# A hybrid encoder block on one core: the norm of attention B from split squares, first loads on two queues, rotary products and splits pinned in program order

## The chip, the cores and the metric

The kernel runs on one core of a Trainium2 chip. The core has five engines with a stream of instructions each: TensorE (PE, matrix products), VectorE (DVE), ScalarE (ACT, functions from tables and casts), GpSimd (POOL) and SyncE (SP, here only the issuing of transfers). Each works through its stream in order and waits for the others by semaphores. The metric is the device time of one execution in microseconds.

## The reference

For a sequence of 512 rows of 1024 numbers: a combined projection, two attention mixers, a gate, an output product and a layer norm (LN1), then an MLP and a second norm. What the change touches is cut out here.

```
proj = x @ w_in -> q_a | k_a | v_a | q_b | k_b | v_b | gate logits
A: 8 heads of 64, chunked softmax attention with a relative bias
B: 4 heads; partial_rope on q_b and k_b (16 of 64 columns, with cos and sin);
   p = softmax(q1 k1^T) - lam * softmax(q2 k2^T), 128-row blocks, causal by chunks
   out = p @ v                                       # 128 columns a head
   out = out * rsqrt(mean(out^2) + 1e-5) * g * (1 - lam_init)
mix = (sigmoid(g_a) * (o_a @ w_a) + sigmoid(g_b) * (o_b @ w_b)) @ w_out
x = LN1(alpha * x + mix)
x = LN2(alpha * x + relu(x @ w_ff1)^2 @ w_ff2)
```

All is float32, and the products have to keep more than one pass of the fast float type (FR, fp32r) gives. So each operand is split in a high part h (a cast by ACT) and the rest l = src - h (a subtraction, mostly by DVE), and a product is three passes: h h, h l, l h.

## The kernel before

**Tiles and stages.** x comes transposed, in eight tiles of 128x512 (X, split into h and l). The weights are streamed in 512 KB chunks (`raw`), each split into `wh` and `wl`. `prefetch(n_dma, n_split)` issues the loads up to chunk n_dma and the splits up to n_split; `chunk()` hands out the next one. `s_group` multiplies four row tiles by 512 columns of weights, `t_pair` makes the transposed product. PE's work on weights comes from the generator `proj`; two more generators, `attn_a` and `attn_b`, give the steps of the attentions, and the main program interleaves them: 36 steps of A with one step of `proj` each, then the steps of B with 1.8 steps of `proj` each.

**Order.** A scheduler gives each engine its order from the dependences and its own estimates. It may move an instruction ahead of others, unless `tc.keep_in_program_order` holds that instruction at its place in the program.

**Attention B.** Each of the four heads has four units, t = 0 to 3, of 128 to 512 key columns. In a unit, `scores` (L270, L271) makes two score maps, DVE adds the mask and finds the maximum (L278), ACT takes the exponential with its row sum (L280), DVE the reciprocal of the sum (L282) and that times lambda (L574); POOL multiplies the second map (L575), and DVE subtracts (L576). PE transposes the result three units later (L289). After unit t = 1 the program has `rope` for q and k of the next head, four POOL products each (L480 to L485), and after t = 2 `prep_b`, in which PE transposes that head's q and k, four blocks each (L492). A unit's scores thus follow on the previous head's `prep_b`.

**The norm of B.** `pv` makes a head's output o (transposed, 128 dimensions by 512 rows); ACT writes its square (L516) and the gained output og (L518). Three steps later `mean_sq` sums the squares over the dimensions with sixteen narrow f32 matmuls in all (L524), and DVE finds 1/sqrt by three Newton steps on 128x8 tiles (L527 to L538). Six steps later `normalise` has POOL spread the result along diagonals (L547), PE multiplies these by ones, and DVE multiplies og by the product (L554).

**Attention A** has the same units with eight heads, where POOL's product is L372. **LN1** follows on the output product (L178 to L185 in groups named mm, o and st): DVE adds the residual (L735), takes statistics (L739), ACT and DVE normalise (L805, L806), and PE transposes (L817).

Of the kernel before, what the change touches and what calls it, by code (L numbers as in the profile page):

```python
# [9 lines left out]
F32 = mybir.dt.float32  # L10
# [30 lines left out]
def block_kernel(ctx, tc, w, x_t, x, pos, relb, bgate, lq1, lk1, lq2, lk2, subg,  # L41
# [36 lines left out]
    def o_bank():  # L78
        return bank("o")

    def split(src, h, l, eng=None):
# [6 lines left out]
    def load_x(k, cuts=((0, S),)):  # L88
        if k not in x_raw:
            x_raw[k] = e_tile()  # L90
        for lo, hi in cuts:
            nc.sync.dma_start(out=x_raw[k][:, lo:hi], in_=x_t[k * P:(k + 1) * P, lo:hi])

# [11 lines left out]
    dma_at, split_at = [0], [0]  # L105

    def prefetch(n_dma, n_split):
        while dma_at[0] < min(NCH, n_dma):
            i = dma_at[0]
            raws[i] = wp.tile([P, 1024], F32, tag="raw", bufs=3, name=name("raw"))  # L110
            if i == 0:
                for j in range(2):
                    sl = slice(512 * j, 512 * (j + 1))
                    if j == 0:
                        load_x(0, ((0, P),))
                    nc.sync.dma_start(out=raws[i][:, sl], in_=w[i][:, sl])
                    load_x(j, ((P, S),) if j == 0 else ((0, S),))
            else:
                nc.sync.dma_start(out=raws[i], in_=w[i])
            dma_at[0] += 1  # L120
        while split_at[0] < min(NCH, n_split):
            i = split_at[0]
            if i in dest:
                hs, ls = dest[i]
                for j in range(2):
                    split(raws[i][:, 512 * j:512 * (j + 1)], hs[j], ls[j],
                          G if i in on_pool else V)
                parts[i] = (hs, ls)
            else:
                h = wp.tile([P, 1024], FR, tag="wh", bufs=3, name=name("wh"))  # L130
                l = wp.tile([P, 1024], FR, tag="wl", bufs=3, name=name("wl"))
                if i == 0:
# [11 lines left out]
    def chunk(ahead=2):  # L144
        c = next_chunk[0]
        prefetch(c + ahead + 1, c + ahead)
        next_chunk[0] += 1
        return parts.pop(c)
# [6 lines left out]
    ones_r = const.tile([P, P], FR, name="ones_r")  # L155
    A.activation(ones_r, ones, AF.Copy, scale=128.0)
    epst = const.tile([P, 1], F32, name="epst")
# [28 lines left out]

    def s_group(act_h, act_l, evac, before=None, nk=4, tail=1, cut_last=False):

# [12 lines left out]
        for c in range(nk):  # L201
            if before:
                before(c)
            wh, wl = chunk()
# [35 lines left out]
    def warm_up(n):  # L240
        ps = st_bank()
        src = e_tile()
        V.memset(src, 0.0)
        for _ in range(n):
            T.matmul(ps, src[:, 0:P].bitcast(FR), src.bitcast(FR), start=True, stop=True)

# [250 lines left out]
    def attn_b():  # L497
# [3 lines left out]
        for which in range(2):  # L501
            rope(qb[which][0])
        ops[0] = prep_b(0)
        yield

        def pv(h):
# [3 lines left out]
            for j in range(NT):  # L510
# [8 lines left out]
            return og, sq  # L519

        def mean_sq(og, sq):
            ms = mm_bank()
            for t in range(NT):
                T.matmul(ms[:, 2 * t:2 * t + 2], sq[:, t * P:(t + 1) * P], ones[:, 0:2],  # L524
                         start=True, stop=True)
            v, y, a = small(8), small(8), small(8)
            V.tensor_scalar(v, ms[:, 0:8], EPS, None, op0=ALU.add)  # L527
            V.tensor_scalar(y.bitcast(I32), v.bitcast(I32), -0.5, float(0x5f3759df),
                            op0=ALU.mult, op1=ALU.add)
            for _ in range(3):  # L530
                V.scalar_tensor_tensor(out=a, in0=y, scalar=-0.5, in1=y,
                                       op0=ALU.mult, op1=ALU.mult)
                V.tensor_tensor(out=a, in0=a, in1=v, op=ALU.mult)
                V.scalar_tensor_tensor(out=y, in0=a, scalar=1.5, in1=y,
                                       op0=ALU.add, op1=ALU.mult)
            rh, rl = small(8, FR), small(8, FR)
            V.tensor_copy(out=rh, in_=y)
            V.tensor_tensor(out=rl, in0=y, in1=rh.bitcast(F32), op=ALU.subtract)  # L538
            return og, sq, rh, rl

        def normalise(og, a, rh, rl):
            rb = mm_bank()
            for n, part in enumerate((rh, rl)):
                diag = vt()
                r = part.bitcast(F32)
                eye = ident[:, :]
                G.tensor_tensor(out=diag.rearrange("p (t q) -> p t q", q=P),  # L547
                                in0=bass.AP(tensor=eye.tensor, offset=eye.offset,
                                            ap=[eye.ap[0], [0, NT], [1, P]]),
                                in1=bass.AP(tensor=r.tensor, offset=r.offset,  # L550
                                            ap=[r.ap[0], [2, NT], [0, P]]), op=ALU.mult)
                T.matmul(rb, ones_r, diag, start=(n == 0), stop=(n == 1))

            V.tensor_tensor(out=a.rearrange("p (q n) -> p n q", n=NT),  # L554
                            in0=og.rearrange("p (n q) -> p n q", q=P),
                            in1=rb.rearrange("p (n q) -> p n q", q=P), op=ALU.mult)
            h_, l_ = vt(), vt()
            split(a, h_, l_)
            ob_h.append(h_)
            ob_l.append(l_)  # L560

        held = {}
        for i in range(len(units) + LAG + 7):
            if i < len(units):
# [19 lines left out]
            if i >= LAG and i - LAG < len(units):  # L584
# [3 lines left out]
                prob_transpose(ex, t, *bufs[h], mm_bank)  # L588
            for stage in (6, 3, 1):
                k = i - LAG - stage  # L590
                if 0 <= k < len(units) and k % NT == NT - 1:
                    h = units[k][0]
                    if stage == 1:
                        held[h] = pv(h)
                    elif stage == 3:
                        held[h] = mean_sq(*held[h])
                    else:
                        normalise(*held.pop(h))
# [48 lines left out]
    def proj():  # L647
        def before(c):
            if c:
                for k in (2 * c, 2 * c + 1):  # L650
                    load_x(k)
                    split_x(k)
# [9 lines left out]

    A.preload_act_table(AF.Exp)
    warm_up(6)
    prefetch(1, 0)
    rope_angles()
    main = proj()
# [4 lines left out]

    advance(7)
    rope_tables()
# [13 lines left out]
    for _ in range(16 + LAG + 7):  # L688
        next(steps_b, None)
# [145 lines left out]
    for n, _ in enumerate(s_group(mh, ml, evac_res(0))):  # L835
        prefetch(c0 + 5, min(c0 + 3, next_chunk[0] + 3))
# [149 lines left out]
```

## Time and profile before

| | |
|---|---|
| median of three runs | 741.46 us (741.35 to 741.72) |
| profiled execution | 741.43 us |
| its span, first to last instruction | 739.6 us |
| mean granted clock of PE | 0.997 |
| busy: PE, DVE, ACT, POOL | 98%, 57%, 38%, 13% |
| read from memory, written | 71.45 MB, 2.10 MB |

A row of the profile names a line of the kernel, an engine, the operation, the tile written and those read. "Idle before" is the time for which the engine stood still just before those instructions, and the arrow names what ended it. Idle time of an engine for which nobody waits costs nothing.

### The profile page before, as it was taken

How to read it: one execution, taken by the hardware profiler on the slowest of the kernel's cores; microseconds unless marked ns; L12 is line 12 of the kernel's file. 1: busy time of each engine (PE TensorE's matmuls, PEld its weight loads, DVE VectorE, ACT ScalarE, POOL GpSimd, SP SyncE). 2: the span in 40 equal slices, each digit the busy share in tenths (PEclk: the TensorE clock that was granted, in tenths of full speed). 3: DMA queues.
4: the chain of work that ended last, by engine and by line, in shares of the span. 5: the costliest groups of instructions: out<-in, count | busy, mean ns of one | idle time of the engine just before them, and what ended most of it. 6: DMA issues, size and time to landing. Idle time of an engine off the chain costs nothing.

```text
span 739.6 us, 9267 instructions
## 1 busy us (share of the span) xinstructions
PE 725.7 (98%) x3446; PEld 606.0 (82%) x3446; DVE 423.4 (57%) x831; ACT 283.6 (38%) x497; POOL 94.4 (13%) x127
## 2 busy tenths in 40 slices
PE   8999999999999999999999999999999999999995
PEld 6888888878888888888788888888888888888885
DVE  6566655546666764746876886423135655612545
ACT  5565654536565643224363223221212322312200
POOL 0023333550122121143000000000000000000001
PEclk9999999999999999999999999999999999999998
DMA  8553222212332222182502232322223223232302
GB/s 294 197 173 112 85 88 60 83 58 86 121 108 86 86 63 104 62 313 96 190 1 84 87 114 86 115 86 98 102 86 113 86 86 113 86 113 86 115 29 85
DMA packets 26940, 78.34 MB, mean 106 GB/s; under 512 B 4368, under 2 KB 5136, under 8 KB 26896
## 3 DMA queue, kind: packets, MB, share of 16 engines
q1 hardware_dynamic: 26176, 76.71, 31.3%
q10 hardware_dynamic: 720, 1.05, 0.4%
q8 instruction: 27, 0.44, 0.2%
q14 instruction: 17, 0.14, 0.1%
HBM read 71.45 MB, written 2.10 MB: 99 GB/s over the span
## 4 chain that ended last, share of the span: by engine, by line
PE 87%; DVE 4%; POOL 3%; ACT 2%; DMA 2%; issue 1%; SPq 0%; DVEq 0%; ACTq 0%; POOLq 0%
PE mm L178 11%; PE mm L180 11%; PE mm L179 11%; PE mm L183 7%; PE mm L185 7%; PE mm L184 7%; PE st L185 3%; PE st L184 3%; PE st L183 3%; PE st L180 3%; PE st L179 3%; PE st L178 3%; POOL G L629 2%; DMA raw<-in_w_dram 2%; PE st L271 1%; PE o L185 1%
## 5 line engine op out<-in xcount | busy, mean ns | idle before, releaser
L83 DVE TENSOR_TENSOR wl<-raw,wh 128x1024 fp32r<-128x1024 f32 (+1 forms) x115 | 140.2, 1219 | 128.5 <-ACT wh L82 128.4
L82 ACT CAST wh<-raw 128x1024 fp32r<-128x1024 f32 (+1 forms) x115 | 120.0, 1044 | 207.6 <-PE st L185 67.1
L183 PE MATMUL mm<-wh,X 128*128 128x512 f32 (+1 forms) x192 | 77.0, 401 | 1.9 <-ACT X L82 1.6
L178 PE MATMUL mm<-X,wh 128*128 128x512 f32 x192 | 76.9, 401 | 0.0
L179 PE MATMUL mm<-X,wh 128*128 128x512 f32 x192 | 74.9, 390 | 0.0
L180 PE MATMUL mm<-X,wl 128*128 128x512 f32 x192 | 74.9, 390 | 0.0
L184 PE MATMUL mm<-wl,X 128*128 128x512 f32 (+1 forms) x192 | 74.5, 388 | 0.0
L185 PE MATMUL mm<-wh,X 128*128 128x512 f32 (+1 forms) x192 | 74.2, 388 | 0.0
L783 POOL TENSOR_SCALAR s<-s 128x1 f32<-128x1 f32 x1 | 0.4, 409 | 388.8 <-DVE s L767 388.8
L178 PE MATMUL mm<-x1t_h,wh 128*128 128x512 f32 x128 | 49.8, 389 | 0.0
L179 PE MATMUL mm<-x1t_l,wh 128*128 128x512 f32 x128 | 49.8, 389 | 0.0
L180 PE MATMUL mm<-x1t_h,wl 128*128 128x512 f32 x128 | 49.8, 389 | 0.0
L280 ACT ACTIVATE e<-e,s 128x128 f32<-128x128 f32 (+3 forms) x64 | 36.1, 564 | 30.4 <-DVE s L278 30.0
L372 POOL TENSOR_SCALAR e<-e,s 128x128 f32<-128x128 f32 (+3 forms) x32 | 34.7, 1085 | 76.3 <-DVE s L282 76.3
L183 PEld LDWEIGHTS mm<-wh,X 128*128 128x128 f32 x192 | 36.2, 189 | 9.8 <-ACT X L82 2.7
L185 PEld LDWEIGHTS mm<-wh,X 128*128 128x128 f32 x192 | 36.0, 188 | 7.8 <-DVE X L83 0.3
L180 PEld LDWEIGHTS mm<-X,wl 128*128 128x128 f32 x192 | 36.0, 188 | 7.7
L178 PEld LDWEIGHTS mm<-X,wh 128*128 128x128 f32 x192 | 36.1, 188 | 6.9
L184 PEld LDWEIGHTS mm<-wl,X 128*128 128x128 f32 x192 | 36.2, 188 | 6.7 <-DVE wl L83 0.2
L179 PEld LDWEIGHTS mm<-X,wh 128*128 128x128 f32 x192 | 36.2, 188 | 6.5
L82 ACT CAST V<-lt 128x512 fp32r<-128x512 f32 x24 | 14.9, 621 | 62.8 <-DVE lt L858 62.8
L180 PE MATMUL st<-x1t_h,wl 128*128 128x512 f32 (+1 forms) x104 | 38.8, 373 | 0.0
(257 smaller groups left out, 1537.0 us busy)
## 6 DMA issues: line engine op xcount, KB each, us to landing
raw<-in_w_dram SPq DMA_DIRECT2D x119, 512.0 KB, 3.3
q<-q SPq DMA_DIRECT2D x32, 128.0 KB, 2.3
G<-in_relb_dram SPq DMA_DIRECT2D x8, 256.0 KB, 4.2
x<-in_x_dram SPq DMA_DIRECT2D x4, 512.0 KB, 7.6
e<-in_x_t_dram SPq DMA_DIRECT2D x7, 256.0 KB, 6.4
out_dram<-x SPq DMA_DIRECT2D x3, 256.0 KB, 2.0
out_dram<-x ACTq DMA_DIRECT2D x3, 256.0 KB, 2.1
raw<-in_w_dram SPq DMA_DIRECT2D x2, 256.0 KB, 3.2
```

Of the source, the lines that this page charges most:

```text
L82: A.copy(out=h, in_=src)
L83: (eng or V).tensor_tensor(out=l, in0=src, in1=h.bitcast(F32), op=ALU.subtract)
L178: T.matmul(ps, lw_h, rh, start=first, stop=False)
L179: T.matmul(ps, lw_h, rl, start=False, stop=False)
L180: T.matmul(ps, lw_l, rh, start=False, stop=last)
L183: T.matmul(ps, ah, w_h, start=first, stop=False)
L184: T.matmul(ps, ah, w_l, start=False, stop=False)
L185: T.matmul(ps, al, w_h, start=False, stop=last)
L271: T.matmul(ps[:, :n], q2[:, sl], k1[:, :n], start=False, stop=True)
L280: A.activation(e[:, :n], e[:, :n], AF.Exp, bias=nm, scale=-1.0, accum_out=sums)
L372: G.tensor_scalar(ex[:, :n], ex[:, :n], r, None, op0=ALU.mult)
L629: G.tensor_tensor(out=m, in0=m, in1=g, op=ALU.add)
```

## The change

It has four parts.

1. *Norm of B.* `mean_sq` goes. In `pv` ACT squares o twice, once to f32 and once to FR, and DVE subtracts the two (`sq_h`, `sq_l`). `normalise` multiplies these by ones (of 1/128, in FR; one matmul each), which leaves the mean in every partition; ACT takes its square root with the epsilon as bias, and DVE the reciprocal over 128x512. The output product by it goes to a new tile. Exp and Sqrt lie in different table sets, so that ACT loads a table ahead of each change. The step comes three steps after `pv`'s in place of six after the unit, and there are three steps fewer at the end.
2. *First loads.* `first_loads` issues x tiles 0 and 1 from ACT's queue, ahead of its table load, and the halves of chunks 0 and 1 with x tiles 2 and 3 from SP's. Chunk 1 is split in halves too. The matmuls that warm PE up read a 128x128 tile repeatedly. `rope_angles` comes after two steps of `proj`.
3. *Rotary products.* The first of the four products of a `rope` call keeps its program order, and the two calls for head 0 become a step each, at i = 22 and 30.
4. *Splits in LN1.* The chunks needed next are split one by one behind the residual add and norm of each row tile, held in program order.

```
     def split(src, h, l, eng=None):
         A.copy(out=h, in_=src)
-        (eng or V).tensor_tensor(out=l, in0=src, in1=h.bitcast(F32), op=ALU.subtract)
+        i = (eng or V).tensor_tensor(out=l, in0=src, in1=h.bitcast(F32), op=ALU.subtract)
+        if pinned[0]:
+            tc.keep_in_program_order(i)
...
+    def first_loads():
+
+        load_x(0, ((0, P), (P, S)), A)
+        load_x(1, q=A)
+        for i in range(2):
+            raws[i] = wp.tile([P, 1024], F32, tag="raw", bufs=3, name=name("raw"))
+            for j in range(2):
+                sl = slice(512 * j, 512 * (j + 1))
+                nc.sync.dma_start(out=raws[i][:, sl], in_=w[i][:, sl])
+                if i == 1:
+                    load_x(2 + j)
+        dma_at[0] = 2
...
-                if i == 0:
+                if i < 2:
                     for j in range(2):
                         sl = slice(512 * j, 512 * (j + 1))
                         split(raws[i][:, sl], h[:, sl], l[:, sl])
-                        split_x(j)
+                        split_x(2 * i + j)
...
-        G.tensor_tensor(out=a, in0=v[:, :, :, 0:16], in1=cos_t, op=ALU.mult)
+        tc.keep_in_program_order(
+            G.tensor_tensor(out=a, in0=v[:, :, :, 0:16], in1=cos_t, op=ALU.mult))
...
         for which in range(2):
             rope(qb[which][0])
+            yield
         ops[0] = prep_b(0)
         yield
...
-            sq = e_tile()
+            sq, sq_h, sq_l = e_tile(), vt(), vt()
             A.activation(sq, o, AF.Square)
+            A.activation(sq_h, o, AF.Square)
             og = e_tile()
             A.activation(og, o, AF.Copy, scale=g8)
+            V.tensor_tensor(out=sq_l, in0=sq, in1=sq_h.bitcast(F32), op=ALU.subtract)
+            return og, sq, sq_h, sq_l
...
-        def mean_sq(og, sq):
-            ms = mm_bank()
-            for t in range(NT):
-                T.matmul(ms[:, 2 * t:2 * t + 2], sq[:, t * P:(t + 1) * P], ones[:, 0:2],
-                         start=True, stop=True)
...
+        def normalise(og, a, sq_h, sq_l):
             rb = mm_bank()
...
+            for n, part in enumerate((sq_h, sq_l)):
+                T.matmul(rb, ones_r, part, start=(n == 0), stop=(n == 1))
+            A.activation(a, rb, AF.Sqrt, bias=epst)
+            V.reciprocal(a, a)
+
+            b = e_tile()
+            V.tensor_tensor(out=b.rearrange("p (q n) -> p n q", n=NT),
                             in0=og.rearrange("p (n q) -> p n q", q=P),
-                            in1=rb.rearrange("p (n q) -> p n q", q=P), op=ALU.mult)
+                            in1=a.rearrange("p (n q) -> p n q", q=P), op=ALU.mult)
...
-            for stage in (6, 3, 1):
+            for stage in (3, 1):
...
-    A.preload_act_table(AF.Exp)
     warm_up(6)
-    prefetch(1, 0)
-    rope_angles()
+    first_loads()
+    tc.keep_in_program_order(A.preload_act_table(AF.Exp))
...
-        if i == 32:
+        if i in (22, 30, 32):
             next(steps_b)
...
+        pinned[0] = True
+        prefetch(c0 + 7, c0 + 4 + min(s + 1, 3))
+        pinned[0] = False
-    for _ in s_group(mh, ml, fin1, tail=4):
+    for _ in s_group(mh, ml, fin1, tail=4, ahead=0):
```

Line numbers shift with it: of the lines named above, L270/L271 become L278/L279, L278 L286, L280 L288, L282 L290, L372 L380, L480 to L485 L489 to L494, L492 L501, L554 L542, L574 L562, L575 L563, L576 L564, L735 L725, L739 L729, L805 L795, L817 L807.

Two places show the new order. Heads are counted from 0 here. The first is POOL's order in attention B, from unit t = 0 of head 1 on. In a row `e` is the second map of a unit (its column count stands last), `G` a head's q or k, and `s` small tiles. Before:

```order
L575 TENSOR_SCALAR e_2124<-e_2124,s_2131 128x128
L575 TENSOR_SCALAR e_2192<-e_2192,s_2199 128x256
L575 TENSOR_SCALAR e_2248<-e_2248,s_2255 128x384
L575 TENSOR_SCALAR e_2334<-e_2334,s_2341 128x512
L575 TENSOR_SCALAR e_2420<-e_2420,s_2427 128x128
```

And after the change:

```order
L563 TENSOR_SCALAR e_2127<-e_2127,s_2134 128x128
L563 TENSOR_SCALAR e_2195<-e_2195,s_2202 128x256
L489 TENSOR_TENSOR s_2206<-G_1186,cos_t 128x128
L490 TENSOR_TENSOR s_2207<-G_1186,sin_t 128x8x8
L492 TENSOR_TENSOR s_2207<-G_1186,sin_t 128x8x8
L494 TENSOR_TENSOR G_1186<-s_2206,s_2207 128x8x16
L489 TENSOR_TENSOR s_2212<-G_1499,cos_t 128x128
L490 TENSOR_TENSOR s_2213<-G_1499,sin_t 128x8x8
L492 TENSOR_TENSOR s_2213<-G_1499,sin_t 128x8x8
L494 TENSOR_TENSOR G_1499<-s_2212,s_2213 128x8x16
L563 TENSOR_SCALAR e_2251<-e_2251,s_2258 128x384
```

The eight rotary products of the next head, all of which stood ahead of attention B before, now stand behind the product of unit t = 1.

The second place is ACT's order at unit t = 1 of head 2, with the two exponentials of the unit, the casts of transposed maps (`ph`), the gates' function (`G`) and, after the change, the norm of head 0. Before:

```order
L607 ACTIVATE G_2461<-mm_2436,bg 128x512
L280 ACTIVATE e_2466,s_2468<-e_2466,s_2467 128x256
L296 CAST ph_2345<-mm_2499 128x3x128
L280 ACTIVATE e_2476,s_2478<-e_2476,s_2477 128x256
L607 ACTIVATE G_2565<-mm_2540,bg 128x512
```

And after:

```order
L593 ACTIVATE G_2468<-mm_2443,bg 128x512
L288 ACTIVATE e_2473,s_2475<-e_2473,s_2474 128x256
L304 CAST ph_2348<-mm_2506 128x3x128
L538 ACT_TABLE_LOAD
L538 ACTIVATE e_2367<-mm_2512,epst 128x512
L288 ACT_TABLE_LOAD
L288 ACTIVATE e_2483,s_2485<-e_2483,s_2484 128x256
L593 ACTIVATE G_2560<-mm_2535,bg 128x512
```

Two table loads and the square root of the norm now stand between the two exponentials. At the same place DVE's order, with the row-sum reciprocals (L290), the reciprocal of the norm (L539) and the product (L542) ahead of the unit's L562, is this after the change:

```order
L290 RECIPROCAL s_2478<-s_2475 128x1
L286 ISA e_2483,s_2484<-st_2480,maskb 128x256
L286 ISA s_2484 128x1
L305 TENSOR_TENSOR pl_2349<-mm_2506,ph_2348 128x3x128
L539 RECIPROCAL e_2367<-e_2367 128x512
L290 RECIPROCAL s_2488<-s_2485 128x1
L542 TENSOR_TENSOR e_2517<-e_2372,e_2367 128x4x128
L562 TENSOR_SCALAR s_2490<-s_2488,lam 128x1
```

Before, small instructions of `mean_sq` stood there:

```order
L282 RECIPROCAL s_2481<-s_2478 128x1
L528 TENSOR_SCALAR s_2511<-s_2510 128x8
L574 TENSOR_SCALAR s_2483<-s_2481,lam 128x1
L531 SCALAR_TENSOR_TENSOR s_2512<-s_2511 128x8
L533 TENSOR_TENSOR s_2512<-s_2512,s_2510 128x8
```

So L562, which POOL's product waits for, has the two wide instructions of the norm ahead of it.

## Rows read from the trace of the kernel before

**Rows 1.** The page: busy us (share of the span) xinstructions

```profile
PE 725.7 (98%) x3446; PEld 606.0 (82%) x3446; DVE 423.4 (57%) x831; ACT 283.6 (38%) x497; POOL 94.4 (13%) x127
```

**Rows 2.** PE's waits: engine, line, released by: us, times, longest

```profile
PE mm L183 <- ACT X L82: 1.6, 1, 1.6
...
PE st L289 <- POOL e L372: 1.3, 1, 1.3
PE mm L817 <- ACT lt L805: 1.0, 1, 1.0
...
PE o L352 <- DVE pl L297: 0.2, 1, 0.2
```

**Rows 3.** Groups of instructions: count | busy us, mean ns | idle before

```profile
L524 PE MATMUL mm<-ones,e 128*128 128x2 f32 x32 | 3.8, 241 | 0.0
```

**Rows 4.** Timeline, 0 to 13: start us, us, engine, line, tiles [idle before]

```profile
3.41 0.62 ACT L82 CAST wh<-raw 128x512 fp32r<-128x512 f32 x1 [1.08 <-DMA raw<-in_w_dram]
...
10.48 1.04 ACT L82 CAST wh<-raw 128x1024 fp32r<-128x1024 f32 x1 [0.60 <-DMA raw<-in_w_dram]
...
12.10 0.50 PE L183 MATMUL mm<-wh,X 128*128 128x512 f32 x1 [1.61 <-ACT X L82]
```

**Rows 5.** Timeline of POOL, 139 to 156

```profile
144.84 0.46 POOL L480 TENSOR_TENSOR s<-G,cos_t 128x128 f32<-128x128 f32 x1
...
146.47 0.46 POOL L480 TENSOR_TENSOR s<-G,cos_t 128x128 f32<-128x128 f32 x1
...
151.32 0.60 POOL L372 TENSOR_SCALAR e<-e,s 128x128 f32<-128x128 f32 x1
```

**Rows 6.** Timeline of DVE in LN1, 350 to 376

```profile
355.54 2.46 DVE L83 TENSOR_TENSOR wl<-raw,wh 128x1024 fp32r<-128x1024 f32 x2 [0.78 <-ACT wh L82]
...
362.69 1.21 DVE L83 TENSOR_TENSOR wl<-raw,wh 128x1024 fp32r<-128x1024 f32 x1
...
373.73 0.69 DVE L735 SCALAR_TENSOR_TENSOR x<-x,st 128x512 f32<-128x512 f32 x1 [1.48 <-PE st L185]
```

**Rows 7.** Timeline of PE: last scores of t = 1, and L492

```profile
175.96 0.28 PE L271 MATMUL st<-q,q 128*128 128x256 f32 x1
...
181.56 1.03 PE L492 MATMUL mm<-ident,G 128*128 128x128 f32 x8
...
200.84 0.28 PE L271 MATMUL st<-q,q 128*128 128x256 f32 x1
...
204.74 1.03 PE L492 MATMUL mm<-ident,G 128*128 128x128 f32 x8
...
226.41 0.28 PE L271 MATMUL st<-q,q 128*128 128x256 f32 x1
```

**Rows 8.** Timeline of POOL in attention B, 172 to 235

```profile
180.87 0.93 POOL L575 TENSOR_SCALAR e<-e,s 128x256 f32<-128x256 f32 x1 [2.18 <-PE mm L179]
...
204.70 0.93 POOL L575 TENSOR_SCALAR e<-e,s 128x256 f32<-128x256 f32 x1 [4.48 <-PE st L271]
...
230.07 0.92 POOL L575 TENSOR_SCALAR e<-e,s 128x256 f32<-128x256 f32 x1 [5.86 <-DVE s L531]
```

**Rows 9.** Timeline of ACT at a table load, 21 to 25

```profile
22.74 1.28 ACT L429 ACT_TABLE_LOAD   x1 [2.79 <-DVE ld L421]
24.03 0.32 ACT L429 ACTIVATE cos_t<-ld,halfpi 128x32 f32<-128x32 f32 x1
```

**Rows 10.** Timeline of ACT, second exponential of t = 1, head 2

```profile
228.83 0.51 ACT L280 ACTIVATE e<-e,s 128x256 f32<-128x256 f32 x1 [0.31 <-DVE s L278]
```

**Rows 11.** Groups of instructions on DVE with 128x512 elements

```profile
L858 DVE TENSOR_TENSOR lt<-lt 128x512 f32<-128x512 f32 x32 | 22.1, 692 | 1.1
...
L554 DVE TENSOR_TENSOR e<-e,mm 128x512 f32<-128x512 f32 x4 | 4.2, 1062 | 0.0
```

**Rows 12.** Timeline of PE, its last matmul

```profile
731.41 0.28 PE L185 MATMUL o<-wh,X 128*128 128x256 f32 x1
```

**Rows 13.** Stretches: us, busy of PE to POOL, PE clock, DMA share, GB/s

```profile
735.28:739.60 4.32, 0.00 (x0) 0.00 (x0) 0.98 (x2) 0.00 (x0) 0.64 (x1) 0.50 0.34 113
```

More of the change, by code (lines that the diff above doesn't have):

```diff
@@ L79, in o_bank, with load_x @@
         return bank("o")
+    pinned = [False]
     def split(src, h, l, eng=None):
         A.copy(out=h, in_=src)
-        (eng or V).tensor_tensor(out=l, in0=src, in1=h.bitcast(F32), op=ALU.subtract)
+        i = (eng or V).tensor_tensor(out=l, in0=src, in1=h.bitcast(F32), op=ALU.subtract)
+        if pinned[0]:
+            tc.keep_in_program_order(i)
     xh, xl, x_raw = [], [], {}
-    def load_x(k, cuts=((0, S),)):
-        if k not in x_raw:
-            x_raw[k] = e_tile()
+    def load_x(k, cuts=((0, S),), q=nc.sync):
+        x_raw[k] = e_tile()
         for lo, hi in cuts:
-            nc.sync.dma_start(out=x_raw[k][:, lo:hi], in_=x_t[k * P:(k + 1) * P, lo:hi])
+            q.dma_start(out=x_raw[k][:, lo:hi], in_=x_t[k * P:(k + 1) * P, lo:hi])
     def split_x(k):
@@ L110, in prefetch @@
             raws[i] = wp.tile([P, 1024], F32, tag="raw", bufs=3, name=name("raw"))
-            if i == 0:
[L112 to L119, printed above, removed]
+            nc.sync.dma_start(out=raws[i], in_=w[i])
             dma_at[0] += 1
@@ L145, in chunk @@
         c = next_chunk[0]
-        prefetch(c + ahead + 1, c + ahead)
+        prefetch(c + ahead + 1, c + max(ahead, 1))
         next_chunk[0] += 1
@@ L155, in block_kernel @@
     ones_r = const.tile([P, P], FR, name="ones_r")
-    A.activation(ones_r, ones, AF.Copy, scale=128.0)
     epst = const.tile([P, 1], F32, name="epst")
@@ L185, in smm, with s_group @@
         T.matmul(ps, al, w_h, start=False, stop=last)
-    def s_group(act_h, act_l, evac, before=None, nk=4, tail=1, cut_last=False):
+    def s_group(act_h, act_l, evac, before=None, nk=4, tail=1, cut_last=False, ahead=2):
         jobs = [(s, 0, S) for s in range(NT)]
@@ L203, in s_group @@
                 before(c)
-            wh, wl = chunk()
+            wh, wl = chunk(ahead)
             if c >= nk - tail:
@@ L241, in warm_up @@
         ps = st_bank()
-        src = e_tile()
-        V.memset(src, 0.0)
+        src = e_tile()[:, 0:P].bitcast(FR)
+        V.memset(src.bitcast(F32), 0.0)
+        wide = bass.AP(tensor=src.tensor, offset=src.offset, ap=[src.ap[0], [0, NT], [1, P]])
         for _ in range(n):
-            T.matmul(ps, src[:, 0:P].bitcast(FR), src.bitcast(FR), start=True, stop=True)
+            T.matmul(ps.rearrange("p (a b) -> p a b", b=P), src, wide, start=True, stop=True)
     def stack(ps, scale):
@@ L514, in pv @@
                          stop=(j == NT - 1))
-            sq = e_tile()
+            sq, sq_h, sq_l = e_tile(), vt(), vt()
             A.activation(sq, o, AF.Square)
+            A.activation(sq_h, o, AF.Square)
             og = e_tile()
             A.activation(og, o, AF.Copy, scale=g8)
-            return og, sq
-        def mean_sq(og, sq):
-            ms = mm_bank()
-            for t in range(NT):
-                T.matmul(ms[:, 2 * t:2 * t + 2], sq[:, t * P:(t + 1) * P], ones[:, 0:2],
-                         start=True, stop=True)
[L526 to L539, printed above, removed]
@@ L541, in normalise @@
-        def normalise(og, a, rh, rl):
-            rb = mm_bank()
[L543 to L554, printed above, removed]
+            V.tensor_tensor(out=sq_l, in0=sq, in1=sq_h.bitcast(F32), op=ALU.subtract)
@@ L557, in normalise @@
             h_, l_ = vt(), vt()
-            split(a, h_, l_)
+            split(b, h_, l_)
             ob_h.append(h_)
@@ L562, in attn_b @@
         held = {}
-        for i in range(len(units) + LAG + 7):
+        for i in range(len(units) + LAG + 4):
             if i < len(units):
@@ L648, in before @@
         def before(c):
-            if c:
+            for k in (2 * c + 2, 2 * c + 3):
+                if 0 < c and k < KD:
+                    load_x(k)
+            if c > 1:
                 for k in (2 * c, 2 * c + 1):
-                    load_x(k)
                     split_x(k)
@@ L661, in proj @@
         yield from branch(0, oa_h, oa_l)
-    A.preload_act_table(AF.Exp)
     warm_up(6)
-    prefetch(1, 0)
-    rope_angles()
+    first_loads()
+    tc.keep_in_program_order(A.preload_act_table(AF.Exp))
+    tc.keep_in_program_order(A.activation(ones_r, ones, AF.Copy, scale=1.0))
     main = proj()
@@ L671, in advance @@
             next(main, None)
-    advance(7)
+    advance(2)
+    rope_angles()
+    advance(5)
     rope_tables()
@@ L687, in block_kernel @@
     due = 0.0
-    for _ in range(16 + LAG + 7):
+    for _ in range(16 + LAG + 4):
         next(steps_b, None)
@@ L835, in block_kernel @@
     for n, _ in enumerate(s_group(mh, ml, evac_res(0))):
-        prefetch(c0 + 5, min(c0 + 3, next_chunk[0] + 3))
+        prefetch(c0 + 5, min(c0 + 4, next_chunk[0] + 3))
     fin = evac_res(1)
```

3 lines of the change are left out of this document (removed).

## Prediction

> **What bounds the kernel now.** I read the busy table first: TensorE (PE) is busy for 98% of the span [rows 1], so a cost or a gain on another engine counts only where PE waits for it. The view of PE's waits comes second, since it lists nearly all the time that can be won without taking work off PE: 1.6 us at the start, for ScalarE's (ACT) cast of an X tile; 1.3 us in attention A, where the transposes L289 wait for a POOL product L372, with 0.2 us at L352 behind it; 1.0 us in LN1, where L817 waits for ACT's L805 [rows 2]. Third, the timeline around each, for what was queued ahead of the late instruction. Last, the order of the changed program, read against the trace where PE will wait for an engine for which it does not wait now. All times below are those of the profiled execution, 741.43 us (a span of 739.6 and 1.83 around it); that is 0.03 below the median of 741.46.
>
> **Mean square on PE (the norm).** Sixteen f32 matmuls with two columns leave PE, 3.8 us busy in 32 records [rows 3]. Each record lasts 241 ns, but they overlap; the last of each of the four groups shows some 0.14 us under the next matmul, so PE moves on by about 3.8 - 4 x 0.14 = 3.2 us. The eight matmuls with ones_r stay, with squares in place of the diagonal products. **-3.2** (bounds -2.8 and -3.8).
>
> **Start.** In the trace before ACT takes the second half-megabyte cast of weights at 10.48, before the X tile that PE needs; PE restarts at 12.10 after 1.61 us idle [rows 4]. Afterwards chunk 1 comes in halves with X2 and X3 among them, and X0 and X1 go by ACT's queue. Between 3.41, when the first 256 KB chunk half is in use, and 10.48, 1792 KB more arrive: 253 KB per us. Up to X2 the new order moves 1280 KB behind the first half, so it is there at about 3.41 + 5.1 = 8.5, and with its cast and one of 0.62 ahead at about 9.7, while PE asks at 12.10 - 1.61 = 10.5. The wait goes, -1.6. Against it, three DMA issues and then the table load stand on ACT ahead of the first cast, which makes that cast some 0.2 us later; the matmul behind the old wait began slowly (0.50 long), which gives about as much back. **-1.6** (bounds -0.8, if X2 is a microsecond late, and -2.0).
>
> **Rotary products of head 0.** Eight groups of four POOL products stand in one burst; a group takes 146.47 - 144.84 = 1.63 us. L372 (128x128), for which PE waits, starts at 151.32 in the midst of them [rows 5]. Spread by the new calls to two other places (steps 22 and 30), and with heads 1 to 3 gone from the burst, nothing stands ahead of L372: **-1.5** (1.3 + 0.2; bounds -1.0 and -1.9, the gap on PE with its slow restart).
>
> **Splits in LN1.** Two splits of 2.46 us together stand ahead of the four residual adds, and another of 1.21 at 362.69, ahead of the add that ends in L805 [rows 6]. Pinned one by one, they fall into pauses of DVE like the 1.48 us at 373.73, which hold one split. **-1.0** (bounds -0.5 and -1.2).
>
> These four make -7.3 (-5.1 to -8.9 with all bounds at once; I take -6.3 to -8.0).
>
> **What waits anew.** In the changed order POOL does the rotary products of head h + 1 behind L563, the product with 256 columns of head h's second unit (before: L575). PE's transposes of that head, L501 (before: L492), wait for POOL, and stand shortly behind the scores of the unit that follows. In the program before they waited for nobody, having been rotated some 27 to 80 us earlier [rows 5, 7]. The heads count from 0, and head 0's transposes are ready long before. For each of the others it is one subtraction. POOL's L563 ends where L575 ends in the trace; the products for q and k end 2 x 1.63 = 3.26 us later; PE would reach the transposes for k 0.4 us after those for q, whose place the trace has, except for head 3, whose transposes are moved.
> - Head 1: L575 ends at 180.87 + 0.93 = 181.80 [rows 8], k is ready at 185.06; PE is there at 181.56 + 0.4 = 181.96 [rows 7]. 3.1 us.
> - Head 2: 204.70 + 0.93 = 205.63, k at 208.89; PE at 205.14. 3.75 us.
> - Head 3: PE. From 175.96 to 181.56 it passes 256 + 21 x 512 + 4 x 384 columns, 0.446 ns each. The changed order has 16,768 columns between the scores of that unit and the transposes for q: with the last score from 226.41 for 0.11 us, PE is there at 234.0, and at k's 0.46 later. POOL: L575 ended at 230.99. But the norm of head 0 now stands on ACT between the two exponentials of this very unit, so L563 is later by a table load of 1.28, a Sqrt for which I take a cast of the same shape, 0.62, and a second load of 1.28, less the 0.31 us that ACT was idle there [rows 4, 9, 10]; and DVE's multiply L542 of 1.06 (L554 before) [rows 11] stands ahead of L562: 3.9. L563 ends at 234.9, k is ready at 238.2. 3.7 us.
>
> Together **+10.5**. None of it is covered, since PE is in order and nothing ahead of L501 is left over. Bounds: the chain up to L575 took 5.6, 4.5 and 4.3 us from the end of the scores, so its scatter of about 1.3 us is what crowding on ACT and DVE costs; 1.3 less for each head gives +6.6, and 1.3 more for head 3 with two more microseconds of its norm gives +14.
>
> **What costs nothing.** The reciprocal with 512 columns isn't in the trace; the nearest row is a DVE operation of the same shape, 0.69 us [rows 11], and the bounds are nothing and the 1.21 of a 1024-wide split [rows 6]. I take 0.69: in head 3's chain it lies under the second table load, and elsewhere on a DVE that is busy for little over half the span. Four more Squares, four Sqrts and six more table loads (7.7 us in all) run on an ACT that has far more slack than that, except where named. The thirteen small DVE operations per head and the eight POOL products of the norm, now gone, were off PE's path and give nothing. Without that cover, when the last head's norm is late, each microsecond of it would be one of PE.
>
> **Two rules of the Trainium skill.** In the trace, the load at 22.74 ends at 24.02, and its function starts at 24.03 [rows 9]: no gap. "ScalarE: Activation LUTs", section "What ACT_TABLE_LOAD costs", has a drain of about 1380 ns beside each load of 1283 ns. The load agrees; by the page's sum the two switches would make head 3's chain 2.8 us longer, and the sum 747.4; a drain that lies ahead of the load would not show in that row. "VectorE: DVE Perf Modes", section "First, the fixed hardware budget", says that Reciprocal divides iteratively with a repeat count of 8; an estimate by the page, eight times a plain pass over 512 columns, would be over 4 us, and the sum some 2 us above mine. No row here shows a wide one.
>
> **Sum.** 741.43 - 7.3 + 10.5 = **744.6 us**.
>
> **Rivals.**
> 1. *The rotary products are ready sooner.* The place is POOL's queue ahead of L501. If the units run less crowded (ACT and DVE lose the 13 small operations and the splits move), L563 ends sooner, and each head is worth its part. For: the scatter of 1.3 us. Against: L575's chain is the same instructions, and k's products alone need 3.26 us of a distance of 3.6 in head 2. The point from which it decides is 1.1 us less for each head: the three waits are then 7.3, the savings. With 2.2 us less for each head they are about 4, and the time 738; with none of them left, 734.1. Chance 0.22 for all below -0.2%, 0.2 for the cases close to nothing.
> 2. *PE's clock falls in the waits.* At the end it falls to half (0.50 in the stretch from 735.28), 3.6 us after the last matmul, which ends at 731.69 [rows 12, 13]; the 1.6 us at 10.5 left it up. The new waits are pairs of about 2.5 and 1.2 us with four transposes between, so in between these. If it fell in one to three of them, and stayed low for as long as it took to fall there, each costs half of 3.6, 1.8 us: 746.4 to 750.0. Chance 0.1.
> 3. *A norm that holds up head 3 longer.* If each of the two switches costs ACT twice the load in its row, head 3's wait grows by 2.6 us, to 747.2; if DVE's wide reciprocal lasts as long as three splits of 1.21 instead of 0.69, by some 1.6, since 1.3 of it lies under the second load and the exponential: 746.2; by both, 748.8. Against: after the load ACT goes on without a gap [rows 9]. Chance 0.1. The two pages of the Trainium skill named above speak for these two cases.
> 4. *The savings don't come* (the start, say, finds another late tile): each left out adds 1.0 to 1.6: to 746 or 747. Within my range.
>
> The forecast itself, 743 to 746.3, has 0.38. I call a difference of under 0.2% (1.5 us) none, which is what a measurement here can tell. Faster 0.22, same 0.20, slower 0.58. For 8 in 10 the range is 737.5 to 749; of the likeliest case alone 743 to 746.3.
>
> **What would show it.** Right: in PE's waits, three pairs at L501 for POOL, about 2 and 1.2 us each; the waits for X, L380 (before L372) and L795 (before L805) gone; no rows of L524. Wrong in the size: L563 256 wide ending under 3.5 us behind its scores. Wrong altogether: no wait for POOL at L501, and a time near 734.

## The result and the profile after

| | median | ratio to before, 95% interval |
|---|---|---|
| before | 741.59 us (5 runs) | |
| after | 752.65 us (752.05 to 753.73, 5 runs) | 1.0151 (1.0136 to 1.0166) |

The change makes the kernel 1.5% slower. I had forecast slower, at 744.6 with a range up to 749: the sign came out, the size did not. The profiled execution of the changed kernel took 753.73 us (span 751.9), the highest of its five, so 1.08 of what follows is more than the median shows.

PE's waits after the change, which answer to [rows 2] (line and engine, released by: us in total, times, longest):

```profile
PE mm L501 <- POOL G L494: 8.6, 5, 2.7
PE st L278 <- DVE s L286: 1.4, 1, 1.4
PE mm L190 <- ACT X L84: 1.4, 2, 0.8
PE st L253 <- DVE e L250: 1.0, 1, 1.0
PE mm L190 <- DVE q L263: 0.3, 1, 0.3
```

The waits of attention A and LN1 are gone, and the forecast wait of the transposes for POOL leads the list. At the start the wait at 10 us is gone too, but two new ones for X (L190, 1.4 us) stand among the first matmuls. The new waits in attention B add up to 8.6 + 1.4 = 10.0 us; I had 10.5. What I had put among the rivals is in the view by stretches (us, then busy of PE, its weight loads, DVE, ACT and POOL, then PE's granted clock, DMA share, GB/s), for the three stretches between the start and the last matmul in which the clock is not at full:

```profile
186.36:189.77 3.41, 3.41 (x11) 2.83 (x12) 2.53 (x6) 1.36 (x4) 1.24 (x1) 0.50 0.68 175
213.66:217.08 3.42, 2.85 (x11) 2.66 (x12) 0.91 (x2) 1.07 (x3) 0.45 (x1) 0.50 0.39 84
247.80:254.62 6.82, 5.78 (x19) 4.79 (x20) 3.85 (x12) 3.38 (x7) 3.53 (x7) 0.50 0.18 38
```

In 13.65 us the clock is at 0.50, 1.2 GHz of 2.4, where before it was at full. PE is busy for 12.04 of them, and work done at half speed would have taken half the time: about 6 us. Together with 10.0 of waits that is 16. Where the whole difference of 12.55 us arises is read from four matmuls that both programs have, by their starts:

| matmul | before | after | later by | in this stage |
|---|---|---|---|---|
| first of the group after the first weights (L178, L185) | 28.54 | 30.68 | 2.14 | +2.14 start |
| last of attention A (L352, L360) | 168.05 | 168.24 | 0.20 | -1.94 attention A |
| last transposes of LN1 (L817, L807) | 385.27 | 397.81 | 12.54 | +12.34 attention B to LN1 |
| last of all | 731.41 | 743.96 | 12.55 | 0 |

The third stage also holds the gains: 3.2 us of narrow matmuls, and LN1's 1.1 (its first L807 now follows the matmul ahead without a gap). So the new waits and what they do to the clock cost 12.34 + 4.3 = 16.6.

The transposes of head 1 on PE (start us, us, engine, line, tiles, idle before and releaser), which answer to 181.56 in [rows 7]:

```profile
181.59 0.33 PE L279 MATMUL st<-q,q 128*128 128x384 f32 x1
184.66 0.65 PE L501 MATMUL mm<-ident,G 128*128 128x128 f32 x4 [2.73 <-POOL G L494]
186.28 1.08 PE L501 MATMUL mm<-ident,G 128*128 128x128 f32 x4 [0.97 <-POOL G L494]
187.01 0.78 PE L185 MATMUL mm<-X,wh 128*128 128x512 f32 x1
187.59 0.63 PE L186 MATMUL mm<-X,wh 128*128 128x512 f32 x1
188.01 0.63 PE L187 MATMUL mm<-X,wl 128*128 128x512 f32 x1
188.44 0.63 PE L185 MATMUL mm<-X,wh 128*128 128x512 f32 x1
...
189.72 0.42 PE L185 MATMUL mm<-X,wh 128*128 128x512 f32 x1
189.98 0.40 PE L186 MATMUL mm<-X,wh 128*128 128x512 f32 x1
```

The pair of waits is there, 2.73 and 0.97. Behind it, from 187.59 on, matmuls start 0.43 us apart, until 189.77, and 0.23 apart afterwards. POOL, for the three heads, answering to [rows 8]:

```profile
181.06 0.92 POOL L563 TENSOR_SCALAR e<-e,s 128x256 f32<-128x256 f32 x1 [2.18 <-PE mm L186]
...
185.77 0.46 POOL L494 TENSOR_TENSOR G<-s,s 128x128 f32<-128x128 f32 x1
...
209.94 0.93 POOL L563 TENSOR_SCALAR e<-e,s 128x256 f32<-128x256 f32 x1 [5.24 <-DVE s L562]
...
213.72 0.45 POOL L494 TENSOR_TENSOR G<-s,s 128x128 f32<-128x128 f32 x1
...
245.66 0.92 POOL L563 TENSOR_SCALAR e<-e,s 128x256 f32<-128x256 f32 x1 [11.74 <-DVE s L562]
...
249.87 0.45 POOL L494 TENSOR_TENSOR G<-s,s 128x128 f32<-128x128 f32 x1
```

By the ends of the scores (176.4, 207.1 and 237.1), L563 ends 5.6, 3.8 and 9.5 us behind them; before it was 5.6, 4.5 and 4.3. In head 1 the addition L494 for q, from 183.21, took 1.39 us in place of 0.46, which made that wait longer. That is not chance: a subtraction of weights (L85) ran on DVE from 183.08 for 1.22 us, and the last section has the like from the other profiles. Head 3's chain, on ACT and then on DVE, is this:

```profile
238.97 1.28 ACT L538 ACT_TABLE_LOAD   x1
240.26 0.69 ACT L538 ACTIVATE e<-mm,epst 128x512 f32<-128x512 f32 x1
240.97 1.28 ACT L288 ACT_TABLE_LOAD   x1
242.26 0.51 ACT L288 ACTIVATE e<-e,s 128x256 f32<-128x256 f32 x1
```

```profile
240.99 3.35 DVE L539 RECIPROCAL e<-e 128x512 f32<-128x512 f32 x1 [1.35 <-ACT e L538]
244.26 0.10 DVE L290 RECIPROCAL s<-s 128x1 f32<-128x1 f32 x1
244.37 1.06 DVE L542 TENSOR_TENSOR e<-e,e 128x512 f32<-128x512 f32 x1
245.28 0.19 DVE L562 TENSOR_SCALAR s<-s,lam 128x1 f32<-128x1 f32 x1
```

The chain is the one forecast, with the loads and the square root between two exponentials. One member is off: the reciprocal takes 3.35 us, not 0.69, and ends 1.5 us after the exponential's sum is there (242.87). So POOL's L563 starts at 245.66, and PE also waits 1.4 us for L286, queued on DVE behind L562.

The start, on PE, answering to the last row of [rows 4]:

```profile
1.04 2.93 PE L253 MATMUL st<-e 128*128 128x512 f32 x6 [1.04 <-DVE e L250]
4.75 0.80 PE L190 MATMUL mm<-wh,X 128*128 128x512 f32 x1 [0.77 <-ACT X L84]
6.14 0.79 PE L190 MATMUL mm<-wh,X 128*128 128x512 f32 x1 [0.60 <-ACT X L84]
...
11.85 0.59 PE L192 MATMUL mm<-wh,X 128*128 128x512 f32 x1
12.28 0.40 PE L190 MATMUL mm<-wh,X 128*128 128x512 f32 x1
```

Where the kernel before waited at 10 us, PE goes on. But its matmuls start 0.43 us apart until 12.28, where in the kernel before they were 0.23 apart from 4.84 on.

### The profile page after: what moved, and what is told of

Same layout as the page of the kernel before. It is cut to its first block, busy times and chain, and to the rows that moved or that the text cites. A ratio compares the mean times of both kernels' runs of the same rounds, so it can differ in the third digit from the quotient of the medians.

```text
span 751.9 us, 9157 instructions
## 1 busy us (share of the span) xinstructions
PE 731.2 (97%) x3414; PEld 609.3 (81%) x3414; DVE 431.9 (57%) x788; ACT 296.4 (39%) x512; POOL 86.1 (11%) x119
## 4 chain that ended last, share of the span: by engine, by line
PE 93%; DVE 2%; POOL 2%; ACT 1%; DMA 1%; issue 1%; DVEq 0%; ACTq 0%; POOLq 0%
PE mm L185 11%; PE mm L186 11%; PE mm L187 11%; PE mm L190 8%; PE mm L191 8%; PE mm L192 8%; PE st L192 4%; PE st L191 4%; PE st L190 4%; PE st L187 3%; PE st L186 3%; PE st L185 3%; PE o L192 1%; PE o L191 1%; PE o L190 1%; PE st L297 1%
## 5 line engine op out<-in xcount | busy, mean ns | idle before, releaser
L85 DVE TENSOR_TENSOR wl<-raw,wh 128x1024 fp32r<-128x1024 f32 (+1 forms) x116 | 139.6, 1204 | 133.3 <-ACT wh L84 133.3
L190 PE MATMUL mm<-wh,X 128*128 128x512 f32 (+1 forms) x192 | 78.1, 407 | 1.7 <-ACT X L84 1.4
L185 PE MATMUL mm<-X,wh 128*128 128x512 f32 x192 | 78.2, 407 | 0.0
L186 PE MATMUL mm<-X,wh 128*128 128x512 f32 x192 | 76.2, 397 | 0.0
L192 PE MATMUL mm<-wh,X 128*128 128x512 f32 (+1 forms) x192 | 75.6, 394 | 0.0
L185 PE MATMUL mm<-x1t_h,wh 128*128 128x512 f32 x128 | 49.8, 389 | 0.0
L288 ACT ACTIVATE e<-e,s 128x128 f32<-128x128 f32 (+3 forms) x64 | 36.0, 563 | 24.1 <-DVE s L286 22.7
L190 PEld LDWEIGHTS mm<-wh,X 128*128 128x128 f32 x192 | 36.9, 192 | 10.0 <-ACT X L84 2.6
L380 POOL TENSOR_SCALAR e<-e,s 128x128 f32<-128x128 f32 (+3 forms) x32 | 34.7, 1085 | 87.6 <-DVE s L290 87.6
L185 PEld LDWEIGHTS mm<-X,wh 128*128 128x128 f32 x192 | 37.2, 194 | 7.2
L186 PEld LDWEIGHTS mm<-X,wh 128*128 128x128 f32 x192 | 36.9, 192 | 6.9
```

What stands on the lines that cost most here:

```text
L85: i = (eng or V).tensor_tensor(out=l, in0=src, in1=h.bitcast(F32), op=ALU.subtract)
L185: T.matmul(ps, lw_h, rh, start=first, stop=False)
L186: T.matmul(ps, lw_h, rl, start=False, stop=False)
L190: T.matmul(ps, ah, w_h, start=first, stop=False)
L192: T.matmul(ps, al, w_h, start=False, stop=last)
L288: A.activation(e[:, :n], e[:, :n], AF.Exp, bias=nm, scale=-1.0, accum_out=sums)
```

## The experiments

Theory after the result: PE waits in heads 1 to 3 for the rotary products, because these stand on POOL behind L563; in these waits its clock falls; the norm lengthens head 3's wait; and at the start the gaps hold the clock down. Each kernel was timed in five rounds beside the kernel before. The last column is from each kernel's profile: the time from the last matmul of attention A to the last transposes of LN1, which leaves out what happens at the start (the kernel before has 217.2 there, the changed one 229.6).

| kernel | median us | ratio, 95% interval | attention A to LN1 |
|---|---|---|---|
| before with the rotary part alone | 750.88 | 1.0116 (1.0099 to 1.0133) | 228.8 |
| before with the norm alone | 738.85 | 0.9956 (0.9940 to 0.9972) | 213.7 |
| before with the first loads alone | 742.58 | 1.0005 (0.9996 to 1.0015) | 217.9 |
| before with the LN1 splits alone | 740.40 | 0.9980 (0.9971 to 0.9989) | 216.1 |
| after without the rotary part | 737.80 | 0.9953 (0.9940 to 0.9965) | 213.2 |
| after without the norm | 750.49 | 1.0109 (1.0092 to 1.0125) | 227.6 |
| after, rotary products behind t = 0 | 736.48 | 0.9934 (0.9922 to 0.9947) | 214.1 |
| after with matmuls in the waits | 748.81 | 1.0105 (1.0090 to 1.0121) | 226.9 |
| after with nine warming matmuls | 751.65 | 1.0141 (1.0128 to 1.0155) | 231.0 |
| after with a copy for the reciprocal | 751.77 | 1.0129 (1.0114 to 1.0144) | 228.7 |
| behind t = 0, nine matmuls | 735.61 | 0.9911 (0.9896 to 0.9926) | 214.0 |
| the same, reciprocal in four | 736.22 | 0.9919 (0.9904 to 0.9934) | 214.1 |

**Each part alone.** The diffs are those of the parts in the section on the change. The rotary part:

> The kernel before with the rotary products pinned and nothing else of the change. Theory (waits for POOL, and a clock that falls in them): the waits of heads 1 and 2 at the transposes come, some 3.7 us each with the clock at half for 3.4 us behind each (1.5 us more each); head 3 has 7.2 us between the t = 1 scores and its transposes here and waits hardly at all; the wait for L372 goes (-1.9). About 749 to 750. Rival (the norm's table loads make the loss): under 741.

```profile
PE mm L493 <- POOL G L486: 6.4, 4, 2.8
...
PE mm L819 <- ACT lt L807: 0.8, 1, 0.8
```

Measured 750.88, a ratio of 1.0116: the loss, as expected, and in two heads only (L493 is the transposes' line there; four waits, two for each head). LN1's wait stays. The clock is at 0.50 for 3.4 and 6.8 us in it.

> The kernel before with the norm from split squares and nothing else of the change. Theory: the sixteen narrow matmuls go, the added work on ACT and DVE is hidden, 738.3 (-3.2), no wait for POOL at the transposes, clock at full throughout. Rival (table loads, square root and wide reciprocal hold up the units): slower than 742, with waits of PE at scores or transposed maps in heads 2 and 3.

The norm alone gains 3.3 us, and PE does not wait for POOL's rotary products. One new wait is there, 0.7 us for DVE at L289 in the unit with the reciprocal; LN1's wait happens to be 0.7 us shorter.

> The kernel before with the first loads on two queues and nothing else of the change. Theory: the wait for X at 10 us goes (-1.8), but the gaps before the first matmuls keep the clock at half until about 12 us (+3.7 to +4): about 743.5. Rival (the start is as forecast, the late clock is chance): 739.9.

742.58 with a ratio whose interval holds 1: between the theory and its rival. In the profiled execution the clock rose at 9.3 us, not 12. Of the 1.2 us that its last matmul is late, 0.5 arise at the start and 0.6 in a longer wait of LN1's.

> The kernel before with the splits in LN1 pinned and nothing else of the change. Both theories: the wait of L817 goes, -1.1: 740.4.

As expected. The four alone sum up to -3.3 + 0.4 + 8.6 - 1.5 = +4.2 us; together they are +11.2 (1.51% of 741.6). Seven microseconds, give or take some two by the intervals, thus belong to no part by itself; in the last column it is 4.7 (12.4 for 11.6 - 3.5 + 0.7 - 1.1).

**Which two parts belong together.**

```
-        tc.keep_in_program_order(
-            G.tensor_tensor(out=a, in0=v[:, :, :, 0:16], in1=cos_t, op=ALU.mult))
+        G.tensor_tensor(out=a, in0=v[:, :, :, 0:16], in1=cos_t, op=ALU.mult)
...
-        if i in (22, 30, 32):
+        if i == 32:
```

> The changed kernel with the rotary products as before (no pin, both calls for head 0 at i = 32). Theory: the three waits at the transposes and the three falls of the clock behind them go together (-15.3), the wait for L372 is back (+1.9): 739.3, clock at full from 13 us on. Rival (the norm makes part of the falls by itself): above 741 with waits left in heads 2 and 3.

737.80: the ratio falls from 1.0151 to 0.9953, by 2.0% or 14.7 us, with no low clock behind the start and L372's old wait back at 1.3 us. From attention A to LN1 it takes 16.3 us less than the changed kernel, close to the 16 of waits and clock above. The rival falls.

The changed kernel with `mean_sq` and `normalise` as before:

> The changed kernel with the norm of before; loads, rotary products and LN1 splits as changed. Theory (pin and norm together make head 3's wait: alone neither does): no wait in head 3 (4.7 us) and no fall of the clock there (some 1.7 us), the narrow matmuls back (+3.2): 749.4. Rival (head 3 waits for the pinned products alone, as heads 1 and 2 do): 755.8.

```profile
PE mm L501 <- POOL G L494: 6.0, 4, 2.7
```

```profile
240.07 0.92 POOL L585 TENSOR_SCALAR e<-e,s 128x256 f32<-128x256 f32 x1 [6.58 <-DVE s L541]
```

1.0109 against 1.0151: the norm costs 3.1 us in this company where it gains 3.3 alone, a swing of 6.4 us. Head 3 has no wait, and PE is busy from 240 to 260 without a pause: the product of the unit (L585 here, L563 above) ends 4.3 us behind its scores, as before the change, and not 9.5. From attention A to LN1 the swing is 5.5 us (2.0 lost in company, 3.5 gained alone); the rest may be the start's, where the profile without the norm has the earlier rise of the clock (9.2 for 12.3). So what belongs to no part by itself is head 3's: the norm's table loads, root and reciprocal in a chain that the pin put on PE's path.

**Where the products stand.**

```
-                if t == 1 and h < 3:
+                if t == 0 and h < 3:
```

> The changed kernel with the pinned rotary products of the next head one unit earlier, behind unit t = 0. Theory (POOL's queue ahead of the transposes decides, not the pin as such): the products end about 0.3 us behind PE's place in head 1 and ahead of it in heads 2 and 3, so at most a short wait is left: 737.5 to 738. Rival (the pinned products hold up L563 itself and the units behind it): waits of PE for POOL at other lines, above 741.

```profile
180.18 1.08 PE L501 MATMUL mm<-ident,G 128*128 128x128 f32 x8
...
203.48 1.33 PE L501 MATMUL mm<-ident,G 128*128 128x128 f32 x8
```

These are PE's transposes of heads 1 and 2: no idle before either. 736.48; the rival falls. The pin itself is harmless, its place one unit too late was the loss. One wait is left in attention B, 1.2 us at L297 in head 2, for DVE's L305 in the unit with the reciprocal.

**The clock.** Matmuls that nobody reads, into the bank that the transposes overwrite:

```
             ps = mm_bank()
+            for _ in range((8, 4)[which] if h else 0):
+                T.matmul(ps, xh[0][:, 0:P], xh[0], start=True, stop=True)
             for t in range(NT):
```

> The changed kernel with added matmuls that nobody reads ahead of the transposes of heads 1 to 3: eight of 128x512 before q's, four before k's, 2.7 us a head, in time in which PE waited. Theory (the clock falls because PE stands still): the transposes come no sooner, but the clock stays up, and the time falls by the 4 to 5 us of matmuls at half clock: about 748. Rival (the clock falls for another reason, or its fall costs nothing): 752 to 753, or more by what the added matmuls take.

PE's timeline at heads 1 and 2 (here L501 are the added matmuls, L503 the transposes), then the one stretch with a low clock:

```profile
178.50 2.02 PE L501 MATMUL mm<-X 128*128 128x512 f32 x8
181.42 0.66 PE L503 MATMUL mm<-ident,G 128*128 128x128 f32 x4 [0.90 <-POOL G L494]
181.83 1.18 PE L501 MATMUL mm<-X 128*128 128x512 f32 x4
183.05 0.66 PE L503 MATMUL mm<-ident,G 128*128 128x128 f32 x4
205.85 2.02 PE L501 MATMUL mm<-X 128*128 128x512 f32 x8
```

```profile
243.64:247.06 3.42, 3.29 (x13) 2.63 (x12) 2.32 (x5) 2.61 (x6) 1.71 (x3) 0.50 0.35 77
```

Thirty-six added matmuls make the kernel 3.4 us faster (1.0105 for 1.0151). The clock stays up in heads 1 and 2, and falls once in head 3, where 2.59 us of standing still were left. The added work and the waits left are 8.2 + 3.5 us, 1.7 more than the 10.0 of waits, so the gain can only be in the speed of the work. Some of it is the start's, where the clock rose early in this profile (4.7). But from attention A to LN1, which leaves the start out, 2.7 us are gained too: PE is busy at the low clock for 8.8 us less (3.3 for 12.0), which is worth 4.4, and 4.4 - 1.7 is 2.7. The theory holds; the forecast of 4 to 5 us was too high by the added work.

**The start.** `warm_up(6)` becomes `warm_up(9)`:

> The changed kernel with nine instead of six matmuls ahead of the first loads, so that PE has work until the first cast is done. Theory (the gaps at 4.0 and 5.5 us keep the clock low until 12.3 us): full clock from about 5 us, -3.3: 749.3. Rival (the clock's rise at 12.3 hangs on the second gap alone, or on chance): within 0.5 of 752.6.

The clock did as expected, the time did not. In the profile the clock rose at 4.2 us, and the first group after the start began at 27.70 in place of 30.68. But the clock was low for 17.1 us in attention B instead of 13.7, and the ratio moved by 0.1% only (0.7 us), within the intervals. The -3.3 is refuted as a change of the median, a smaller gain is neither shown nor excluded. What decides it is seen across the profiled executions of all kernels:

| start of the kernel | clock rises at | first L178 or L185 at |
|---|---|---|
| before's (before, and the rotary, norm and LN1 parts alone) | 4.8, 5.9, 6.3, 5.2 | 28.54, 28.10, 29.03, 29.14 |
| changed, six matmuls (copy, matmuls in the waits, without rotary, without norm, loads alone, behind t = 0, after) | 4.3, 4.7, 8.7, 9.2, 9.3, 9.4, 12.3 | 28.24, 27.47, 28.80, 29.07, 29.06, 29.10, 30.68 |
| changed, nine (after, behind t = 0, with the reciprocal in four) | 4.2, 5.6, 6.5 | 27.70, 28.28, 28.95 |

With a rise up to 5.6 the changed start is 0.3 to 1.1 us ahead of that in the trace before; from the two earliest rises with six matmuls to the latest, each microsecond by which the clock rises later costs 0.3 to 0.4 us. With six matmuls and their pauses it rose later than 8 us in five of seven profiles, with nine or the start of before in none of seven: that the pauses matter is likely. "TensorE: Matmul & The Clock Gate" in the Trainium skill, section "What's actually happening", says that the number of slow matmuls at a kernel's start varies between runs of the same kernel; the second column agrees that the rise is partly chance. Executions without a profile don't show theirs.

**The reciprocal.** `V.reciprocal(a, a)` becomes `V.tensor_copy(out=a, in_=a)`, which leaves out the division:

> The changed kernel with a copy of the same size in place of the wide reciprocal, so that the norm multiplies by the root in place of dividing by it. Theory (the reciprocal of 3.35 us outlasts the second table load and exponential in head 3's chain by 1.4 us): L563 of that unit 1.4 us sooner behind its scores, PE's wait for L286 nearly gone: 751.2. Rival (table loads alone set that chain): within 0.5 of 752.6.

```profile
239.49 0.43 DVE L539 COPY e<-e 128x512 f32<-128x512 f32 x1 [1.35 <-ACT e L538]
239.95 1.08 DVE L542 TENSOR_TENSOR e<-e,e 128x512 f32<-128x512 f32 x1
...
241.41 0.16 DVE L290 RECIPROCAL s<-s 128x1 f32<-128x1 f32 x1 [0.38 <-ACT e L288]
241.60 0.21 DVE L562 TENSOR_SCALAR s<-s,lam 128x1 f32<-128x1 f32 x1
```

L562 now waits for ACT, not for DVE's wide operation, L563 ends 7.8 us behind its scores instead of 9.5, and the wait for L286 is gone. But PE's waits in head 3 are 3.5 us for 3.7, and while its low clock lasts 3.4 us instead of 6.8, head 1's lasts 6.8 instead of 3.4:

```profile
181.76:188.59 6.83, 5.76 (x17) 4.59 (x18) 3.80 (x10) 2.37 (x5) 3.21 (x6) 0.50 0.57 154
```

The ratio is 0.22% lower (1.6 us, for 1.4 expected), but the two intervals overlap, and from attention A to LN1 the profile gains 0.8 us only, while its start, with the clock up at 4.3, is 2.4 us sooner. That the reciprocal lengthens the chain is shown; what it costs in time is not.

**Towards a better version.**

> The changed kernel with the rotary products behind unit t = 0 and nine matmuls ahead of the loads. Theory (the clock rises near 4.3 us with nine, it rose at 9.4 with six): -2.4 against the 736.5 with six: 734.1. Rival (the rise is chance): 736 to 737.

735.61, a ratio of 0.9911, is faster than both kernels, and lies between the theory and its rival; against six matmuls (0.9934) the intervals just overlap. In the profile the first group begins 0.8 us sooner (28.28 for 29.10), and all behind it takes as long.

> As the one with both edits, and the wide reciprocal in four pieces of 128 columns, between which DVE can do others' work. Theory (the remaining 1.4 us of PE's wait for L305 in head 2 comes from DVE's 3.35 us in one piece): -0.5 to -1 against that kernel. Rival (the multiply behind it holds up the unit as before): no difference.

```profile
PE mm L297 <- DVE pl L305: 1.3, 1, 1.3
```

No difference; the wait for L305 is as long as with one piece. But three of the four pieces ran back to back (230.00 to 232.58), with one small operation ahead of the fourth, and L305 starts where it did (238.12, 238.15 with one piece and six matmuls). So the edit let hardly anything in between; what holds up L305 stays open.

## Why the prediction was wrong in size

- *Mean square off PE, -3.2.* Right: the norm alone gives -3.3.
- *Rotary burst, -1.5.* Right in place, -1.94 measured over attention A in the profile; the slow matmuls behind the wait were only in my bound.
- *LN1, -1.0.* Right: -1.5 alone (its interval reaches from -0.8 to -2.2), and no gap ahead of L807.
- *Start, -1.6.* The step that named the late tile was right. "Some 0.2 us later" for the first cast was too little. The load of the table ends at 3.41, not 2.00, and the cast that PE waits for starts 0.47 us later (3.88). I had not followed what a longer pause ahead of the first matmuls may do to the clock, though the trace before has it at full from 4.84 on; how much of the late rise is the pause and how much chance stays open. In the profiled execution the start is 2.14 later instead of 1.6 sooner; in medians of the part alone it is +0.4. This term was off by 2 us in the median and 3.7 in the profile.
- *New waits, +10.5.* Right in mechanism and in the sum: 10.0, the sum in part by luck, since errors of either sign met in it. Head 1 had 3.70 for 3.1 (the slow addition; the burst from which I took 1.63 us for a group also has groups of 2.5, which I passed over), head 2 2.67 for 3.75 (L563 came 0.7 us sooner, which is rival 1 in part), head 3 3.7 for 3.7, 1.42 of it at L278. Head 3's chain was longer than I took, since the reciprocal lasted 3.35 us and not 0.69, above my bound of 1.21 (the second case of my rival 3, which gave it three splits of 1.21); some of that hides in the wait at L278 and in matmuls at half clock between the waits. That bound failed: a wide row of another operation says nothing of a divide. The Trainium skill's "VectorE: DVE Perf Modes", section "First, the fixed hardware budget", had it nearer: its iterative divide made an estimate of over 4 us, and the trace has 3.35. The other page, "ScalarE: Activation LUTs", section "What ACT_TABLE_LOAD costs", is not borne out in its drain: the cast ahead of the load ends at 238.95, the load lasts from 238.97 for 1.28 us, and the root starts at 240.26.
- *The clock in the waits.* This is the step that failed. The sum priced the waits at their length and held nothing for the clock; I had that as a rival with a chance of 0.1 and up to 5.4 us. It fell in all three heads, 13.65 us in all, worth about 6, and the matmuls added into the waits show that it is the waits that bring it about. I argued from the 1.6 us at 10.5, which left the clock up, and from a fall 3.6 us after the last matmul; I placed a pair of waits, 2.5 and 1.2 with four small transposes between, between the two, and still held the fall to be unlikely. I also took all low stretches to be 3.6 us long; they last 3.4 or 6.8, and which of the two varies from profile to profile.

The profiled execution is 9.1 us above the forecast. The clock in the waits is 6 of that and the start 3.7 (+2.1 for -1.6); the other terms together are about half a microsecond the other way. Without the clock's part in the waits the time (752.65 - 6) would have been inside my range.

## What to carry to other kernels

An instruction pinned in an in-order queue is as late as the latest thing ahead of it there: before pinning, subtract the end of that thing from the place of the consumer, and move the pin one step earlier if the difference is small. Where PE would stand still for microseconds and again soon after, add the clock to the price (here 6 us beside 10 of waits), and look at pauses among a kernel's first matmuls in the same way. A change that gains alone can lose beside another, when that one puts a chain on the path that the first lengthens (the norm here: 3.3 us gained alone, 3.1 lost beside the pin), so time pairs as well as parts. And where a start varies from execution to execution, as here, compare kernels by the stage that the edit touches, beside the whole time.

## What the runs showed of the hardware beyond that

- DVE's reciprocal of 128x512 takes 3.35 us; a copy of the same shape and type takes 0.43, a subtraction 0.69.
- At 0.50 of its clock PE starts matmuls with 512 columns 0.427 us apart, and 0.227 at full.
- A rotary product on POOL that begins while DVE does a subtraction of weights (L83 or L85 here, two tiles of 128x1024) takes 1.3 to 1.5 us in place of 0.3 to 0.5, and ends 0.2 to 0.3 us after it. That is so in all fourteen profiles, without an exception; in the kernel before, 1.35 us from 141.76, beside L83 from 141.57 for 1.23.
- Waits of 1.71 and 0.96 us with four transposes between were enough for the clock to fall (head 2, at 213.66); 1.61 us at 10.5 us in the kernel before, and 1.22 us at 237.7 us in the one with the products behind t = 0, were not.
